# Seven block products for the second feed-forward's gate and up tiles, with the residual held in DRAM

## The chip, the cores and the metric

The kernel runs on one core of a Trainium2 chip. The metric is the device time of one execution in microseconds; of several executions the median is taken.

## The reference

One decoder layer for T = 1092 columns (1024 prompt tokens, 64 sample tokens, 4 zero columns), width 1024, in float32:

```
h = x + 0.5 * g1 * SwiGLU_1(rms(x) * (1 + sc1) + sh1)
u = rms(h) * (1 + sc2) + sh2
h = h + g2 * mixer(u)                  # attention and state space branches, then @ w_out
h = h + 0.5 * g3 * SwiGLU_2(rms(h) * (1 + sc3) + sh3)
y = final_rms(h)

def swiglu(u, w_in, w_out):            # w_in 1024 x 5632, w_out 2816 x 1024
    g, up = split(u @ w_in, 2)
    return (silu(g) * up) @ w_out
```

The change concerns SwiGLU_2 and the join between the mixer and it.

## The kernel before, in words

Activations lie with features on the 128 partitions and the columns in the free dimension. Every float32 operand of a large product is scaled by a power of two and split into two fp16 parts, hi and lo (`split`, L92: hi on ScalarE at L94, lo on VectorE at L95). A product of a 128-feature tile runs three passes per k-tile: hi x hi, hi x lo, lo x hi. The columns go in three chunks of CH = 364 (the last takes 360 after the first pass), so a `unit` (L165, matmuls at L171) over nk k-tiles is 9 nk matmuls of some 363 columns into one PSUM tile.

`Weights` (L99) walks a fixed list of weight groups: `fetch` issues the DMA of a group into one of two buffers `wf` (L114, on SP's queue), `measure` reduces its absolute maximum on VectorE (L88), GpSimd spreads that over the partitions (L81), and `split` makes `wh` and `wl`, of which there are two buffers each. A group is split one step ahead of its use and loaded and measured two ahead.

A feed-forward (`ffn`, L376) has 22 tiles of hidden features. `up(i)` (L382) makes one: two units of 8 k-tiles (gate, then up), 144 matmuls; ScalarE takes the silu of the gate (L387), VectorE multiplies (L390) and reduces the tile's maximum for the later split. The first two tiles (`up_two`, L400, matmuls at L181) go chunk by chunk of the columns, since the modulated norm arrives in chunks. Hidden tiles are grouped by PARTS = ((0,11),(11,18),(18,22)); `halves` splits a part, `down` (L436) multiplies it with w_out and adds to the residual `x`, which stays in SBUF; `last_part` (L461) does the last four k-tiles chunk by chunk and calls `after_chunk` for each.

Before the second feed-forward, `mixer_b` (L1211) multiplies the two branches, merges them and applies w_out: a first half with `unit`, and `last_part` for the second, whose `after_chunk` computes the reciprocal root mean square (`rstd_chunk`, L277, a chain of thirteen small VectorE operations) and `modulate_chunk` (L309: VectorE L322, ScalarE L325 and L327, VectorE L327 for each part of the eight k-tiles). The order of instructions on each engine is that of the program with a scheduler's priorities; each engine executes its own list in order.

Of the kernel before, what the change touches and what calls it, by code (L numbers as in the profile page):

```python
# [20 lines left out]
P = 128  # L21
# [4 lines left out]
PARTS = ((0, 11), (11, 18), (18, 22))  # L26
# [6 lines left out]
T = 3 * CH  # L33
EPS = 1e-6
# [14 lines left out]
class K:  # L49
    """State shared by the parts of the kernel."""  # L50


class Pool:
    """A tile pool whose tiles are named after their tags."""
# [14 lines left out]
def pow2_scale(k, m, pool=None, tag="sc", bufs=8):  # L69
# [4 lines left out]
    nc.vector.tensor_scalar(sc[:, 1:2], sc[:, 1:2], 2.0 ** -100, 2.0 ** -14, op0=ALU.max, op1=ALU.mult)  # L74
    nc.vector.reciprocal(sc[:, 0:1], sc[:, 1:2])
    return sc[:, 0:1], sc[:, 1:2]
# [15 lines left out]
def split(k, hi, lo, src, s):  # L92
    """hi + lo = s * src to 22 bits."""
# [5 lines left out]
class Weights:  # L99
    """The groups of weights in the order in which they are used: split one ahead, loaded and measured two ahead.  # L100
    The last group of a product, of twice the size, is kept in slots of the scope's own, aside from the ring."""
# [5 lines left out]
    def fetch(self):  # L107
        k = self.k
        src, nk, nm, *aside = self.order.pop(0)
        wf = []  # L110
        for part in [src[:, :nk // 2], src[:, nk // 2:]] if aside else [src]:
# [3 lines left out]
        self.fetched.append((wf, nm, bool(aside)))  # L115

    def measure(self):
# [5 lines left out]
        m = absmax(k, mx) if aside else mx[:, :1]  # L123
        self.loaded.append((wf, nm, aside, *pow2_scale(k, allmax(k, m))))
# [6 lines left out]
    def split(self):  # L131
        k = self.k
        wf, nm, aside, s, inv = self.loaded.pop(0)
        parts = []
        for f in wf:
# [5 lines left out]

    def ahead(self):
        """To be called when the use of a group ends, or by next()."""
# [16 lines left out]
def width(c, first):  # L160
    """Columns of chunk c that a pass takes: the zeros after the last token only need the first one."""
# [3 lines left out]
def unit(k, w, cols, act, nk):  # L165
    """One output tile: [P, 3, CH] of PSUM = sum over nk k-tiles of w[:, :, cols]^T act."""
# [9 lines left out]
def product(k, ps, w, cols, act, nk, c):  # L176
    """ps [P, CH] = chunk c of the columns of such a tile."""
# [6 lines left out]

def unit_chunk(k, w, cols, act, nk, c, sink, ps=None):
    """Such a chunk in its own bank, for sink(c, ps)."""
# [28 lines left out]
def ada_part(k, dr, part, queue=None, then=None):  # L215
    """mods[:, part * 8 + tile, sequence]: one part of the modulation."""
# [25 lines left out]
def norm_coef(k, i, gain):  # L242
    """Modulation i as u * s = n * A + B, with s a power of two: A, B and 1 / s."""
# [9 lines left out]
    s, inv = pow2_scale(k, allmax(k, bound), k.co, f"ns{i}", 1)  # L253
# [9 lines left out]
def square_sums(k, x, c):  # L263
    """The sums of squares of the columns of chunk c of x [P, KD, T]: PSUM [4 x 32 equal rows, CH / 4]."""
    nc = k.nc
    ss = k.pss.tile([P, 512], F32, tag="s")
    for kt, nk in GROUPS:
        sq = k.tmp()[:, :nk, :]
        nc.scalar.activation(sq, x[:, kt:kt + nk, c * CH:(c + 1) * CH], AF.Square)
# [15 lines left out]
    # the inverse square root: half the exponent's bits, then Newton's steps  # L285
# [16 lines left out]
def normalize_chunk(k, x, c, bc=None):  # L302
    """x[:, :, chunk c] to unit root mean square, in place."""
# [43 lines left out]

def scaled_gate(k, gate, iv):
# [5 lines left out]
def add_gated(k, xm, ps, g):  # L354
    """xm [P, T] += g * ps, g [P, NSQ] by sequence, ps [P, 3, CH]."""
# [1177 lines left out]
```

## Time and profile before

| quantity | value |
|---|---|
| median of three runs | 2511.44 us (2509.38, 2511.44, 2512.85) |
| profiled execution, its span | 2513.7 us |
| TensorE (PE) busy | 2430.5 us, 97%, 16615 matmuls |
| VectorE (DVE) busy | 1417.2 us, 56% |
| ScalarE (ACT) busy | 782.4 us, 31% |
| GpSimd (POOL) busy | 168.2 us, 7% |

The profile is one further execution; the page gives its span, which holds the program from the first instruction to the last, and shows no other time of it. Busy time is summed per engine. A matmul's listed duration holds its passage through the array as well, so the distance between the starts of successive matmuls is what a matmul costs in a stream.

### The profile page before, as it was taken

The numbers are of one execution on the slowest core, as the hardware profiler recorded it, in microseconds if no ns is written. First come the engines' busy times: TensorE is split into PE (matmuls) and PEld (weight loads), VectorE is DVE, ScalarE is ACT, GpSimd is POOL, SyncE is SP. The second block draws the span as 40 slices with busy tenths as digits, with TensorE's granted clock in tenths as the row PEclk, the third lists the DMA queues.
The fourth block names the chain that finished last, engine by engine and source line by source line (L and its number), as shares of the span: only waits on it lengthen the run. The fifth ranks groups of instructions, "written<-read, shape, count | busy, mean of one in ns | idle before, by whom it ended". The sixth has DMA issues, their size and how long they took to land.

```text
span 2513.7 us, 38505 instructions
## 1 busy us (share of the span) xinstructions
PE 2430.5 (97%) x16615; PEld 1456.6 (58%) x16615; DVE 1417.2 (56%) x2637; ACT 782.4 (31%) x905; POOL 168.2 (7%) x249
## 2 busy tenths in 40 slices
PE   6999999999999999999999899999999999999997
PEld 2555566666656565775444444655666656666564
DVE  4522355458676744638889787697333353333545
ACT  3311122111122432146778676324211221111303
POOL 0111000000000000001133200000000000000000
PEclk8999999999999999889999999999999999999999
DMA  9644101112112234444133214520111111111112
GB/s 349 220 184 168 51 24 55 62 62 88 59 57 99 89 98 147 104 149 157 66 110 104 96 41 148 210 68 18 34 51 51 36 47 62 51 48 35 45 35 72
DMA packets 81946, 229.41 MB, mean 91 GB/s; under 512 B 11680, under 2 KB 45856, under 8 KB 72560
## 3 DMA queue, kind: packets, MB, share of 16 engines
q1 hardware_dynamic: 67952, 179.96, 21.0%
q0 software_dynamic: 13376, 46.70, 5.3%
q8 instruction: 130, 2.13, 0.3%
q10 hardware_dynamic: 448, 0.29, 0.1%
q14 instruction: 40, 0.33, 0.0%
HBM read 190.68 MB, written 36.24 MB: 90 GB/s over the span
## 4 chain that ended last, share of the span: by engine, by line
PE 42%; DVE 6%; ACT 4%; issue 2%; DMA 1%; another core or an unknown queue 1%; POOL 0%; DVEq 0%; POOLq 0%; ACTq 0%
PE u L171 27%; PE u L181 8%; PE z L850 2%; PE o L868 1%; PE P L787 1%; DVE mx L88 1%; PE P L863 1%; DVE h L95 1%; DVE wl L95 1%; DMA wf<-in_w_in 0%; ACT tmp L325 0%; DMA wf<-in_w_out_b 0%; ACT ae L857 0%; PE z L911 0%
## 5 line engine op out<-in xcount | busy, mean ns | idle before, releaser
L171 PEld LDWEIGHTS <-wh 128*128 128x128 f16 x6144 | 589.3, 97 | 387.3 <-issue 38.5
L171 PE MATMUL u<-u,wh 128*128 128x364 f16 (+1 forms) x4032 | 740.6, 317 | 0.0
L171 PE MATMUL u<-u,wl 128*128 128x364 f16 (+1 forms) x2016 | 420.1, 315 | 0.0
L181 PE MATMUL u<-u,wh 128*128 128x364 f16 (+1 forms) x1632 | 393.5, 319 | 12.0 <-ACT u L327 6.3
L171 PEld LDWEIGHTS <-wl 128*128 128x128 f16 x3072 | 298.9, 98 | 176.1 <-issue 2.6
L94 ACT ACTIVATE wh<-wf,sc 128x2048 f16<-128x2048 f32 (+3 forms) x92 | 172.1, 1871 | 681.8 <-PE u L171 616.5
L88 DVE TENSOR_REDUCE mx<-wf 128x1 f32<-128x2048 f32 (+3 forms) x98 | 208.7, 2131 | 250.3 <-DMA wf<-in_ffn_w_in 156.6
L171 PE MATMUL u<-h,wh 128*128 128x364 f16 (+1 forms) x1728 | 315.7, 317 | 9.9 <-DVE h L95 6.1
L181 PE MATMUL u<-u,wl 128*128 128x364 f16 (+1 forms) x816 | 260.2, 319 | 1.1 <-DVE wl L95 1.1
L181 PEld LDWEIGHTS <-wh 128*128 128x128 f16 x1824 | 176.5, 98 | 126.0 <-issue 28.6
L390 DVE SCALAR_TENSOR_TENSOR h<-u,iv,sil 128x1092 f32<-128x1092 f32 x40 | 54.2, 1354 | 331.6 <-PE u L171 293.8
L95 DVE SCALAR_TENSOR_TENSOR wl<-wf,sc,wh 128x2048 f16<-128x2048 f32 (+3 forms) x92 | 200.7, 2182 | 47.3 <-ACT wh L94 46.8
L81 POOL PARTITION_ALL_REDUCE am<-mx x106 | 49.4, 472 | 1966.7 <-DVE mx L88 1880.2
L171 PE MATMUL u<-h,wl 128*128 128x364 f16 (+1 forms) x864 | 180.1, 316 | 0.0
L387 ACT ACTIVATE sil<-u,iv 128x1092 f32<-128x1092 f32 x40 | 46.9, 1171 | 385.3 <-PE u L171 385.3
L181 PEld LDWEIGHTS <-wl 128*128 128x128 f16 x912 | 89.4, 98 | 69.8 <-issue 18.5
L181 PEld LDWEIGHTS <-aside 128*128 128x128 f16 x864 | 83.0, 97 | 50.4 <-issue 1.2
L181 PE MATMUL u<-h,aside 128*128 128x364 f16 (+1 forms) x576 | 90.9, 317 | 0.0
L358 DVE SCALAR_TENSOR_TENSOR x<-u,gt,x 128x728 f32<-128x728 f32 x40 | 38.8, 971 | 87.7 <-PE u L171 87.7
L227 PE MATMUL s<-aw,cs 128*32 128x256 f32 x576 | 64.8, 406 | 11.2 <-DMA aw<-in_ada_w 11.1
L857 ACT ACTIVATE ae<-z,bias,csqk 128x512 f32<-128x512 f32 (+3 forms) x96 | 62.9, 666 | 40.7 <-PE z L855 18.8
L858 DVE TENSOR_SCALAR az<-z,csqk,bias 128x512 f32<-128x512 f32 (+3 forms) x96 | 64.4, 674 | 8.8 <-ACT ae L857 8.2
(375 smaller groups left out, 2583.5 us busy)
## 6 DMA issues: line engine op xcount, KB each, us to landing
wf<-in_ffn_w_in SPq DMA_DIRECT2D x44, 1024.0 KB, 4.9
aw<-in_ada_w POOLq DMA_DIRECT2D x56, 512.0 KB, 6.6
wf<-in_w_in SPq DMA_DIRECT2D x16, 1024.0 KB, 5.6
wf<-in_ffn_w_out_a SPq DMA_DIRECT2D x16, 704.0 KB, 4.1
x<-in_xT SPq DMA_DIRECT2D x6, 1456.0 KB, 14.1
sg<-gd SPq DMA_DIRECT2D x16, 546.0 KB, 5.5
aw<-in_ada_w SPq DMA_DIRECT2D x16, 512.0 KB, 8.3
gd<-gate SPq DMA_DIRECT2D x45, 182.0 KB, 1.9
```

The source lines that it names most:

```text
L81: k.nc.gpsimd.partition_all_reduce(r, m, P, ABSMAX)
L88: k.nc.vector.tensor_reduce(m, src, axis=axis, op=ALU.max, apply_absolute_value=True)
L94: r = k.nc.scalar.activation(hi, src, AF.Copy, scale=s)
L95: k.nc.vector.scalar_tensor_tensor(lo, src, s, hi, op0=ALU.mult, op1=ALU.subtract)
L171: k.nc.tensor.matmul(ps[:, c, :n], wt[:, cols], act(kt, part)[:, c * CH:c * CH + n], start=kt == 0 and j == 0, stop=kt == nk - 1 and j == 2)
L181: k.nc.tensor.matmul(ps[:, :n], wt[:, cols], act(kt, part)[:, c * CH:c * CH + n], start=kt == 0 and j == 0, stop=kt == nk - 1 and j == 2)
L227: nc.tensor.matmul(ps[32 * i:32 * i + 32, :], k.cs[:, 4 * kk + j, :], ws[i][:, j, :], start=kk + j == 0, stop=kk == 1 and j == 3)
L387: nc.scalar.activation(c3(sil), pg, AF.Silu, scale=iv)
L390: nc.vector.scalar_tensor_tensor(c3(h), pu, iv, c3(sil), op0=ALU.mult, op1=ALU.mult)
L850: nc.tensor.matmul(ps[:, :n], a[r, P * j:P * j + P], b[r, cols], start=i == 0, stop=True, skip_group_check=True)
L857: nc.scalar.activation(ae[:, h, :n], ps[:, :n], AF.Abs, scale=inv, bias=b)
L858: nc.vector.tensor_scalar(az[:, h, :n], ps[:, :n], inv, b, op0=ALU.mult, op1=ALU.add)
```

## The change

In the second feed-forward each gate and up tile is made from seven products of blocks (Winograd's form of Strassen's scheme): the k-tiles are cut into two halves of four, the columns into two halves of HT = 546, the outputs into gate and up. Each of the seven products has 4 k-tiles x 3 passes over 546 columns, in two matmuls of 272 and 274 columns: 24 matmuls, 168 for a tile where there were 144 of some 363 columns. Sums of products build up in PSUM where they can; the others are added on VectorE (`seven_products`). The weights' sums s1 to s4 are made on VectorE before the split (`Weights.seven`); the group's splits grow from 2048 columns to 2048, 1024 and 512. The activations' sums t1 to t4 are made in `Factors.chunk`, called for each of three chunks of 182 + 182 columns, and take the place of the modulated norm's buffer; the plain blocks lie in a new pool. `x` is stored to DRAM (`xd`) after the mixer, each row comes back for the first `down` and is stored again, and `x` is reloaded before the second. `halves_unit` cuts the columns in two halves for the mixer's branches and the down products, PSUM becomes three tiles of two banks, and PARTS becomes ((0,10),(10,18),(18,22)) for both feed-forwards.

```diff
-PARTS = ((0, 11), (11, 18), (18, 22))
+PARTS = ((0, 10), (10, 18), (18, 22))
...
+    def seven(self, f, s):
+        a11, a12, a22, a21 = (f[:, i:i + 512] for i in range(0, 2048, 512))
...
+        v.tensor_sub(s3, a11, a21)
+        v.tensor_add(a21, a21, a22)
+        v.tensor_sub(s2, a21, a11)
+        v.tensor_sub(s4, a12, s2)
+        h, l = (k.wp.tile([P, 2048], F16, tag=t_, bufs=2) for t_ in ("wh", "wl"))
+        split(k, h, l, f, s)
+        h3, l3 = (k.w3.tile([P, 1536], F16, tag=t_, bufs=2) for t_ in ("w3h", "w3l"))
+        split(k, h3[:, :1024], l3[:, :1024], t[:, :1024], s)
+        split(k, h3[:, 1024:], l3[:, 1024:], s4, s)
...
+def halves_unit(k, w, cols, act, nk):
+    for h in range(2):
+        ps = pair_tile(k)
+        cut = ((240, 512), (512, 786))
...
+    def chunk(self, k, x, coef, c, bc):
...
+        for g in range(4):
...
+            for q in range(2):
+                v.tensor_mul(t[:, q], paired(x, c)[:, 4 * q + g], bch)
...
+            v.tensor_sub(s[:, 0:2], flat[:, 1::2], flat[:, 0:2])
+            v.tensor_sub(s[:, 2], flat[:, 3], s[:, 0])
+            v.tensor_sub(s[:, 3], flat[:, 2], s[:, 2])
+            for src, hi, lo in ((flat[:, 0], ...
+                nc.scalar.activation(hi, src, AF.Copy)
+                v.tensor_sub(lo, src, hi)
...
+def seven_products(k, w, fac, iv, h, lo, hi):
...
+    add(X, "a11", "b11", True)
+    nc.scalar.activation(p1, view(X), AF.Copy)
+    add(Y, "s2", "t2", True)
+    v.tensor_add(u2, view(Y), p1)
+    add(X, "a12", "b21", False)
+    nc.scalar.activation(h1, view(X), AF.Silu, scale=iv)
+    add(Y, "s3", "t3", False)
+    v.tensor_add(u3, view(Y), p1)
+    add(Z, "s1", "t1", True)
+    v.tensor_add(u3, view(Z), u3)
+    add(Y, "a22", "t4", False)
+    v.tensor_add(p1, view(Y), p1)
+    add(Z, "s4", "b22", False)
+    v.tensor_add(h2, view(Z), u2)
+    nc.scalar.activation(h2, h2, AF.Silu, scale=iv)
+    v.scalar_tensor_tensor(hh, q[:, :, :n], iv, hh, op0=ALU.mult, op1=ALU.mult)
...
+    def up_two():
...
+        for lo, hi in ((0, 2 * QT), (2 * QT, HT)):
+            for i in range(2):
+                seven_products(k, ws[i][0], fac, ivs[i], hs[i], lo, hi)
...
+    def row(m):
+        t = k.hp.tile([P, T], F32, tag="h", name="xr")
+        nc.sync.dma_start(t, xd[:, m, :])
+        return t, lambda: nc.sync.dma_start(xd[:, m, :], t)
...
+    for m in range(KD):
+        nc.sync.dma_start(x[:, m, :], xd[:, m, :])
...
+                box["fac"] = Factors(k)
+            box["fac"].chunk(k, x, box["cf"], c, rstd_chunk(k, x, c, pairs=True))
+            nc.sync.dma_start(paired(xd, c), paired(x, c))
```

VectorE's list around one of the later tiles, before (`wf` raw weights, `wl` their lo part, `am` the spread maximum, `h` the hidden tile, L88 maxima):

```order
L390 SCALAR_TENSOR_TENSOR h<-u,iv,sil 128x1092
L88 TENSOR_REDUCE hm<-h 128x1
L95 SCALAR_TENSOR_TENSOR wl<-wf,sc,wh 128x2048
L88 TENSOR_REDUCE mx_17449<-wf 128x1
L73 TENSOR_SCALAR sc<-am 128x1
```

One multiplication, one maximum and one split, and then the maximum of the weights that have just been loaded.

And in the changed kernel, from the last add of a tile's products to the first add (`u2`, printed as u_17933, L494) of the next tile, for which TensorE's next product into the same PSUM tile waits (L97 is the lo part of a split, L90 a maximum, L508 the hidden tile):

```order
L503 TENSOR_TENSOR q<-u,q 128x546
L97 SCALAR_TENSOR_TENSOR wl<-wf,sc,wh 128x2048
L505 TENSOR_TENSOR h<-u,u_17721 128x546
L97 SCALAR_TENSOR_TENSOR w3l<-tmp,sc,w3h 128x1024
L508 SCALAR_TENSOR_TENSOR h<-q,iv,h 128x1092
L97 SCALAR_TENSOR_TENSOR w3l<-tmp,sc,w3h 128x512
L90 TENSOR_REDUCE hm<-h 128x1
L90 TENSOR_REDUCE mx_17921<-wf 128x1
L494 TENSOR_TENSOR u_17933<-u,q 128x546
```

Where one product's result and one split stood per tile, there are seven operations between the add that follows the a22 product (L503) and the next tile's `u2`.

VectorE's list at the start of the second feed-forward, before (L327 to L343 finish the last chunk of the norm, L417 multiplies the first two tiles' chunks):

```order
L340 TENSOR_TENSOR tmp<-tmp,B 128x512
L327 TENSOR_TENSOR u<-tmp,u 128x3x296
L343 TENSOR_TENSOR u<-tmp,u 128x8x64
L327 TENSOR_TENSOR u<-tmp,u 128x2x296
L417 SCALAR_TENSOR_TENSOR h<-u,iv,sil 128x364 x4
```

The last chunk's part of the norm is followed at once by the first tiles' multiplications.

And in the changed kernel (L454 to L461 finish the last chunk of the activations' sums and their lo parts, L155 to L158 make the weights' sums of a later tile, L494 is the first tile's first add):

```order
L454 TENSOR_TENSOR tmp<-tmp 128x364
L461 TENSOR_TENSOR f<-tmp,f 128x182
L455 TENSOR_TENSOR tmp<-tmp 128x182
L461 TENSOR_TENSOR f<-tmp,f 128x2x182
L456 TENSOR_TENSOR tmp<-tmp 128x182
L461 TENSOR_TENSOR u<-tmp,u 128x4x182
L155 TENSOR_TENSOR tmp<-wf 128x512
L156 TENSOR_TENSOR wf<-wf 128x512
L157 TENSOR_TENSOR tmp<-wf 128x512
L158 TENSOR_TENSOR tmp<-wf,tmp 128x512
L494 TENSOR_TENSOR u_16661<-u,q 128x364
```

The first tile's first pass takes 364 of each half's 546 columns, which come from the first two chunks; its first add stands behind the last of the third chunk's operations and four weights' sums.

## Rows read from the trace of the kernel before

**Rows 1.** The page: busy time, share of the span and instructions of each engine.
```profile
PE 2430.5 (97%) x16615; PEld 1456.6 (58%) x16615; DVE 1417.2 (56%) x2637; ACT 782.4 (31%) x905; POOL 168.2 (7%) x249
```
**Rows 2.** Windows from the mixer's branches on: us, busy (count) per engine, PEclk, DMA.
```profile
1599.00:1694.70 95.70, 91.92 (x593) 56.90 (x591) 84.37 (x112) 27.50 (x21) 5.38 (x7) 1.00 0.29 100
1694.70:1745.40 50.70, 49.92 (x426) 30.69 (x424) 39.43 (x83) 23.65 (x30) 0.69 (x2) 1.00 0.07 22
1745.40:1794.30 48.90, 47.45 (x357) 29.60 (x357) 20.16 (x37) 14.92 (x22) 0.00 (x0) 1.00 0.04 13
1794.30:2016.40 222.10, 222.10 (x1442) 139.47 (x1441) 76.95 (x92) 36.98 (x26) 4.26 (x12) 1.00 0.13 46
```
**Rows 3.** The chain of waits, 1590 to 2400: start us, us, what.
```profile
1764.66 29.61 PE u L181 x192
1794.27 222.15 PE u L171 x1440
...
2016.51 1.35 DVE h L390
2017.87 1.27 DVE h L95
...
2019.18 345.58 PE u L171 x2229
...
2368.68 7.60 DVE h L95 x6
```
**Rows 4.** Timeline of PE in the mixer's projection: start us, us, instruction.
```profile
1058.85 0.27 PE L1107 MATMUL z<-wl,u 128*128 128x256 f16 x1
...
1059.83 0.27 PE L1107 MATMUL z<-wl,u 128*128 128x256 f16 x1
```
**Rows 5.** Groups by line and shape, ACT, 1580 to 2380: busy us, mean ns, idle.
```profile
L94 ACT ACTIVATE wh<-wf,sc 128x2048 f16<-128x2048 f32 x26 | 52.0, 2001 | 218.5 <-PE u L171 196.9 <-PE u L181 11.5 <-DVE sc L75 10.1
L325 ACT ACTIVATE tmp<-tmp,B,A 128x364 f32<-128x364 f32 x16 | 9.9, 678 | 13.4 <-DVE tmp L322 13.4
```
**Rows 6.** The same view of DVE.
```profile
L95 DVE SCALAR_TENSOR_TENSOR wl<-wf,sc,wh 128x2048 f16<-128x2048 f32 x26 | 60.9, 2344 | 9.3 <-ACT wh L94 9.0
L88 DVE TENSOR_REDUCE mx<-wf 128x1 f32<-128x2048 f32 x26 | 59.4, 2285 | 89.0 <-DMA wf<-in_ffn_w_in 87.9 <-DMA wf<-in_w_out_b 1.1
L88 DVE TENSOR_REDUCE hm<-h 128x1 f32<-128x1092 f32 x22 | 28.4, 1289 | 0.6
L390 DVE SCALAR_TENSOR_TENSOR h<-u,iv,sil 128x1092 f32<-128x1092 f32 x20 | 27.1, 1355 | 185.4 <-PE u L171 185.4
...
L477 DVE SCALAR_TENSOR_TENSOR x<-u,gs,x 128x364 f32<-128x364 f32 x16 | 8.7, 590 | 2.4 <-PE u L181 2.2
...
L290 DVE TENSOR_TENSOR r<-r 128x91 f32<-128x91 f32 x9 | 2.3, 256 | 0.3
...
L295 DVE TENSOR_TENSOR rd<-r,ident 128x364 f32<-128x364 f32 x3 | 1.6, 537 | 0.1
...
L322 DVE TENSOR_TENSOR tmp<-x,s 128x592 f32<-128x592 f32 x1 | 0.8, 762 | 0.0
...
L482 DVE TENSOR_TENSOR st<-u,gs 128x192 f32<-128x192 f32 x2 | 0.7, 351 | 0.0
...
L338 DVE TENSOR_TENSOR tmp<-x,s 128x512 f32<-128x512 f32 x1 | 0.7, 679 | 0.0
```
**Rows 7.** Timeline around one tile's end: SP's DMA issue, then the maximum and its wait.
```profile
1843.77 0.33 SPq L114 DMA_DIRECT2D wf<-in_ffn_w_in  x1
...
1848.60 2.29 DVE L88 TENSOR_REDUCE mx<-wf 128x1 f32<-128x2048 f32 x1 [4.85 <-DMA wf<-in_ffn_w_in]
```
**Rows 8.** Windows of PE around two of its pauses: us, busy (count), PEclk, DMA share, GB/s.
```profile
2016.00:2019.20 3.20, 0.89 (x7) 0.97 0.00 0
2019.20:2021.00 1.80, 1.80 (x7) 0.50 0.00 0
2021.00:2023.00 2.00, 2.00 (x10) 0.65 0.00 0
2384.00:2389.00 5.00, 3.38 (x23) 1.00 0.00 0
```

More of the change, by code (lines that the diff above doesn't have):

```diff
@@ L33 @@
 T = 3 * CH
+HT = T // 2
+QT = HT // 3
 EPS = 1e-6
@@ L49 @@
 class K:
+    pass
 class Pool:
@@ L182, in product, with paired, two, pair_tile @@
                                start=kt == 0 and j == 0, stop=kt == nk - 1 and j == 2)
+def paired(t, c):
+    if len(t.shape) == 2:
+        return t.rearrange("p (h c n) -> p c h n", h=2, c=3)[:, c]
+    return t.rearrange("p k (h c n) -> p k c h n", h=2, c=3)[:, :, c]
+def two(t):
+    return t.rearrange("p (h n) -> p h n", h=2) if len(t.shape) == 2 else t.rearrange("p k (h n) -> p k h n", h=2)
+def pair_tile(k):
+    return k.psu.tile([P, 1024], F32, tag="u", bufs=3)
+def halves_unit(k, w, cols, act, nk):
+    for h in range(2):
+        ps = pair_tile(k)
+        cut = ((240, 512), (512, 786))
+        for kt in range(nk):
+            for j, (wt, part) in enumerate(passes(w, kt)):
+                for a, b in cut:
+                    a0 = h * HT - 240
+                    k.nc.tensor.matmul(ps[:, a:b], wt[:, cols], act(kt, part)[:, a0 + a:a0 + b],
+                                       start=kt == 0 and j == 0, stop=kt == nk - 1 and j == 2)
+        yield h, slice(h * HT, h * HT + HT), ps[:, 240:786]
 def unit_chunk(k, w, cols, act, nk, c, sink, ps=None):
@@ L485, in last_part, with ffn_seven, hidden, up @@
         after_chunk(c)
+def ffn_seven(k, fac, ivu, gate, xd, after_chunk):
+    nc = k.nc
+    hs, hm = {}, {}
+    def hidden(i):
+        p = [a <= i < b for a, b in PARTS].index(True)
+        if p not in hm:
+            hm[p] = k.small.tile([P, 12], F32, tag="hm", bufs=3)
+        j = i - PARTS[p][0]
+        return hm[p][:, j:j + 1]
+    def up(i):
+        w = k.w.next()
+        iv = mul_small(k, w[1], ivu)
+        hs[i] = k.hp.tile([P, T], F32, tag="h")
+        seven_products(k, w[0], fac, iv, hs[i], 0, HT)
+        absmax(k, hs[i], hidden(i))
+    def up_two():
+        ws = [k.w.next() for _ in range(2)]
+        ivs = [mul_small(k, w[1], ivu) for w in ws]
+        for i in range(2):
+            hs[i] = k.hp.tile([P, T], F32, tag="h")
+        for lo, hi in ((0, 2 * QT), (2 * QT, HT)):
+            for i in range(2):
+                seven_products(k, ws[i][0], fac, ivs[i], hs[i], lo, hi)
+        for i in range(2):
+            absmax(k, hs[i], hidden(i))
+    def halves(p):
+        a, b = PARTS[p]
+        s, inv = pow2_scale(k, allmax(k, absmax(k, hm[p][:, :b - a])), tag="sh", bufs=3)
+        parts = []
+        for i in range(a, b):
+            h2 = k.hp.tile([P, 2, T], F16, tag="h")
+            ins = split(k, h2[:, 0, :], h2[:, 1, :], hs[i], s)
+            if i - a < 6:
+                behind = ins
+            parts.append(h2)
+        return lambda kt, part: parts[kt][:, part, :], inv, behind
+    def down(p, hact, inv, behind, rows):
+        nk = PARTS[p][1] - PARTS[p][0]
+        per = 1 + p
+        for m in range(KD):
+            if m % per == 0:
+                if m == 0:
+                    with k.tc.issue_after(behind):
+                        w = k.w.next()
+                else:
+                    w = k.w.next()
+                iv = mul_small(k, w[1], inv)
+            xm, done = rows(m)
+            g = scaled_gate(k, gate[:, m, :], iv)
+            for h, _, ps in halves_unit(k, w, slice(m % per * P, m % per * P + P), hact, nk):
+                add_gated_half(k, xm, h, ps, g)
+            done()
+    def row(m):
+        t = k.hp.tile([P, T], F32, tag="h", name="xr")
+        nc.sync.dma_start(t, xd[:, m, :])
+        return t, lambda: nc.sync.dma_start(xd[:, m, :], t)
+    up_two()
+    for i in range(2, PARTS[0][1] + 1):
+        up(i)
+    down(0, *halves(0), row)
+    for i in range(PARTS[0][1] + 1, NFF):
+        up(i)
+    x = k.up.tile([P, KD, T], F32, tag="u", name="x")
+    for m in range(KD):
+        nc.sync.dma_start(x[:, m, :], xd[:, m, :])
+    h1, h2 = halves(1), halves(2)
+    down(1, *h1, lambda m: (x[:, m, :], lambda: None))
+    last_pairs(k, x, gate, *h2, lambda c: after_chunk(c, x))
```

222 lines of the change are left out of this document (172 added, 50 removed).

## The prediction, made before the changed kernel had run

> **What bounds the kernel now.** The page first: TensorE is busy 97% of the span and VectorE 56% [rows 1], so on average the matmul stream is the bound, and a scheme that needs fewer matmul columns attacks the right engine. Averages hide stages, so next the windows from the mixer's branches on [rows 2]. In the second feed-forward's plain tiles (1794.3 to 2016.4) TensorE is busy without a gap while VectorE works 76.95 of 222.1 us. In the branches and the first half of w_out (1599.0 to 1694.7) VectorE is already busy 84.37 of 95.7 us, and in the next two windows, the chunked product with the norm behind it and the first two tiles, it works 39.43 of 50.7 and 20.16 of 48.9 us: there it is close behind TensorE. The chain of waits says the same: one piece of 222.15 us of matmuls for ten tiles, a break of 2.7 us where the hidden tile and its split end last (2016.51 to 2019.18), then 345.58 us of matmuls [rows 3]. The last column but two of the windows is the granted clock, 1.00 in all of these.
>
> **What TensorE saves.** Ten tiles are 1440 matmuls in 222.15 us: 22.2 us a tile, 154.3 ns for some 363 columns [rows 3]. For 272 or 274 columns no row stands; the nearest are the projection's 256-column matmuls, each with a weight load of its own: nine starts in 0.98 us, 108.9 ns [rows 4]. A line through both gives 0.424 ns a column, almost nothing fixed, and 116.1 ns for 273 columns. A tile of 168 then takes 19.5 us, 2.7 less; for the 20 tiles after the first two **-54 us**. Weight loads (139.47 us for 1441, 97 ns each [rows 2]) still fit behind matmuls of 116 ns. The down products change from 9 x 154.3 to 12 x 116.1 ns a k-tile, 144 k-tiles: +0.6 us.
>
> The Trainium skill, page "TensorE: Matmul & The Clock Gate", section "Back-to-back issue gap", speaks against this: in a stream of weight loads and matmuls it gives about 81 ns for 128 columns and 131 ns for 512. Read linearly that is an estimate of 100 and 112 ns here, so a tile would go from 16.1 to 16.8 us and the change would lose on TensorE itself. The trace does not agree: 363 columns take 154.3 ns, more than the page has for 512, and 256 and 363 columns stand nearly in proportion.
>
> **What VectorE must do in a later tile.** It gets 15 us of work a tile (four adds of 512 columns 2.4, five of 546 columns 3.2, splits 4.1, the hidden product 1.3, two maxima 3.4, small ones 0.8) where it has 7.7 (76.95 us for ten [rows 2]); that would hide under 19.5 us, but the order matters. Take the end of the a22 product as zero. It frees the weights' slot, so ScalarE's `wh` runs until 2.05 (2.00 us [rows 5]). VectorE's list then stands in a row; successive operations start 0.08 us before the listed end of the one ahead (six splits of 1.35 us take 7.60 [rows 3]). `wl` to 4.45 (2.34), h2's add of 546 columns 0.64 net (0.76 at 592), to 5.09; `w3l` of 1024 columns 1.20, to 6.29 (between 0.59 at 364 and 2.34 at 2048); the hidden product 1.27, to 7.56; `w3l` of 512 columns 0.67, to 8.23; the tile's maximum 1.21, to 9.44 [rows 6]. The next weights' DMA starts after `wl` and takes 4.85 us [rows 7], landing at 9.33, in time; their maximum 2.21, to 11.65; then u2's add, to **12.3**. TensorE has four products of 24 matmuls (s4 b22, and the next tile's first three) before it needs that add: 4 x 2.79 = **11.15**. It waits 1.15 us in each such tile. The tiles whose successors' weights are narrow w_out groups are free of it (two before each down product), as is the first, priced below; 15 remain: **+17 us**. Bounds: 0, if the eight operations of this list are 0.15 us shorter each, and 2.3 us a tile if the DMA is late by as much as ScalarE's turn. I take 1.15, which the rows give.
>
> **The join.** Here VectorE loses what TensorE gains.
> - Window 1: two weight groups' sums and extra splits come in: four adds of 512 columns (0.68, net 0.60 [rows 6]) and 1.20 + 0.67, 4.3 us a group, 8.6 for two, and 1 us for operations cut in halves. VectorE is idle 11.3 us of this window; I let half of the addition fall into that: +5.4 (0 to 9.6).
> - From there TensorE's first chunk ends after 16.9 us, a third of 50.7 [rows 2]. Then VectorE is never free until the first u2 add, since its list holds all three chunks' sums ahead of it, though the first pass only needs two. A chunk's sums are four groups of two multiplications of 364 (0.46 net each), adds of 364, 182 and 182 (0.46, 0.27, 0.27) and lo parts of 182, 364 and 728 (0.27, 0.46, about 0.84) [rows 6]: 3.5 us a group, 14 a chunk, 16 in the third with the sample columns. Before, the norm took some 7. With three root-mean-square chains (thirteen operations at 0.25, the first exposed at some 6 us), two chunks' residual adds (eight at 0.52, some more for samples: 4.5 and 5) and four weights' adds: 6 + 14 + 4.5 + 3.3 + 14 + 5 + 3.3 + 16 + 3 = 69 us. ScalarE has 3.5 us a group as well (0.68 for one 364 [rows 5]; two of those and three conversions) in alternation with VectorE's; I allow 10 us for the two waiting for each other (2 to 18). The u2 add ends 96 us after window 1.
> - TensorE has done 36 matmuls of the first pass by then and waits. What is left: 132 at 154.7, 20.4 us; 168 of 182 columns, between 77 ns by the line and 97 by their weight loads, 14.6 us; a wait of 2.5 in the second pass, where a weight split (`wl` 2.3 and `w3l`) stands ahead of the second tile's add. After a pause of 2.7 us the clock was granted at 0.50 and came back after some 3 us, a loss of 1.6 us, while a pause of 1.6 us left it at 1.00 [rows 8]; this pause is longer, so +1.6. That is 39 us.
> - 96 + 39 = 135 against 99.6 before: +36, with window 1 **+41 us** (29 to 55).
>
> **Small terms.** The third tile's weights are split late: +2. At the break before the first down product, an add of 0.64 and a silu of some 0.7 join the 2.7 us chain: +1.2. The last chunk's paired output: +0.5. Storing and reloading x runs on SP's queue while TensorE works: the first row is needed only after a half-unit of 7 us, and weights' loads behind it are two groups ahead; 0, or about 5 us (one load's 4.85 [rows 7]) if a row comes late at either down product. The waits of 1.15 us are shorter than the pause that left the clock alone, so they cost no clock. FFN 1's new parts: 0.
>
> **The sum.** -54 + 17 + 41 + 0.6 + 2 + 1.2 + 0.5 = +8 us on the profiled span of 2513.7, which lies 2.3 above the median of the runs: 2511.4 + 8 = 2520, and with the x traffic's bound in view I say **2521 us**, slower by 0.4%. Below 0.2%, or 5 us, a measurement cannot tell a change.
>
> **Rivals.**
> - *VectorE keeps up* (faster). If u2's add ends before 11.15 in the later tiles, the 17 us fall away, and if VectorE and ScalarE interleave well the join costs 32: 2521 - 17 - 9 = 2495. It decides at 1.15 us in a list of 12.3. For it: VectorE idles some 4 us of every tile in my walk, behind `wh` and the products. Against: its list is in order and the wait for `wh` is given by the slots. Chance 0.20.
> - *One of the two comes out well*: 2504 or 2512. Chance 0.17.
> - *The waits cost clock.* If each is 2.6 us in place of 1.15, the clock falls to 0.50 as after the 2.7 us pause: 1.45 + 1.6 us in 15 tiles, 46 us: 2567. For it: a DMA or ScalarE 1.4 us late suffices. Chance 0.08.
> - *Seven products are no fewer.* If matmuls of 273 columns do not start every 116 but every 131 ns, 168 of them take 22.0 us, as the 144 did. VectorE's wait vanishes too: 2521 + 50 - 17 = 2554. The proportion of rows 3 and 4 speaks against it. The page named above has a rule of this kind. Chance 0.05.
>
> **How the numbers follow.** My forecast has 0.50, with a range of its own of 2510 to 2538 from the join's bounds; 2521 is its middle. Faster by over 0.2% (below 2506.4): the first rival and a little of the second, 0.23. Within: the rest of the second and the forecast's low end, 0.19. Slower: 0.58. For eight in ten the range goes from 2494, the first rival's time, to 2545, where the join's upper bound ends; the two dear rivals and half of the cheap one stay outside.
>
> **What would show it.** Right: matmuls of 272 and 274 columns start about 116 ns apart; in the list of waits PE waits for DVE at L494 some 1.2 us a tile, and a tile takes 20.6 us; between the end of the w_out product and the first two tiles PE pauses for 20 us or more, released by the L494 add, and VectorE is full meanwhile; the later tiles begin some 41 us later than before. Wrong: tiles of 19.5 us without a wait (first rival), a granted clock below 1.00 in the later tiles (third), a spacing well above 116 (fourth), or waits of PE at the down products for the adds that need x.

## Result, and the profile after

| | us |
|---|---|
| changed kernel, median of 6 runs | 2525.93 (2521.8 to 2534.3) |
| kernel before, same chip, 6 runs | 2511.68 (2509.38 to 2519.49) |
| ratio, 95% interval | 1.0058 [1.0038, 1.0078] |
| span of the profiled execution | 2522.0, before 2513.7: +8.3 |

The change makes the kernel slower by 0.6%. The forecast was 2521 us, slower, and +8 us on the profiled span. The direction is right and the two spans differ as forecast, but the medians differ by 14.2 us (13.7 in the repeat below), so the change costs more than I said. The terms agree less well still, as shown below.

The page's first line now (it answers to [rows 1]): TensorE has 44 us less, VectorE 194 us more.

```profile
PE 2386.3 (95%) x17863; PEld 1577.3 (63%) x17863; DVE 1611.6 (64%) x3008; ACT 850.8 (34%) x1029; POOL 163.4 (6%) x249
```

What TensorE waited for, 1480 us to the end, changed kernel: engine and line that waited, who released it, total us, times, longest.

```profile
PE u L481 <- ACT q L491: 18.6, 2, 18.2
PE u L481 <- DVE u L494: 12.6, 17, 2.3
PE u L237 <- DMA ob<-od: 12.4, 2, 11.5
```

These three lines are the largest of the change's new waits. The first is one pause of 18.2 us in the join; the second 0.7 us in each of most later tiles; the third, at the start of the mixer's branches, is nowhere in the prediction.

The chain of waits of the changed kernel (it answers to [rows 3]): start, us, what.

```profile
1709.47 14.87 PE u L539 x96
...
1949.84 19.77 PE u L481 x167
1969.62 19.89 PE u L481 x168
...
2029.09 105.19 PE u L237 x898
...
2163.30 8.28 PE u L481 x69
...
2183.89 8.28 PE u L481 x69
...
2204.46 8.28 PE u L481 x69
...
2361.18 89.81 PE u L237 x768
2451.00 14.60 PE u L539 x95
```

Three marks split the path: the last half of w_out begins at 1709.47 (before: 1694.9), the third tile of the second feed-forward at 1837.1 (before: 1794.27 [rows 3]), the last half of the last product at 2451.00 (before: 2446.3). A tile for which the list shows no wait takes 19.9 us, 118.4 ns a matmul (19.89 us for 168); with its wait a tile recurs every 20.58 us (2163.30, 2183.89, 2204.46). The 20 tiles and their down products take 613.9 us where they took 652.0, a gain of 38.1; everything ahead of them had already lost 42.8. The third tile has no clean start: 19 of its matmuls run ahead of the mark, and twelve of the second tile's with a wait of 1.4 us behind it, which come to 2.2 and 2.3 us and nearly cancel.

The 118.4 ns still hold a piece of the wait. In a tile without a listed wait `u2` ends at 1969.57, and the product that needs it starts at 1969.62, 0.40 us after the start of the last two matmuls ahead of it, where two otherwise take 0.23:

```profile
1968.85 0.72 DVE L494 TENSOR_TENSOR u<-u,q 128x546 f32<-128x546 f32 x1
1969.22 0.39 PE L481 MATMUL u<-f,wl 128*128 128x272 f16 x2
1969.62 0.63 PE L481 MATMUL u<-u,w3h 128*128 128x272 f16 x4
```

The 0.16 us too much lie within the last matmul's listed duration and so in no list of waits. A tile without any wait takes 19.7 us, as a run below shows.

Windows of the changed kernel (columns as in [rows 2]): the join up to TensorE's restart, the last 6 us of that, the rest of the first two tiles, and the following tiles.

```profile
1709.40:1803.00 93.60, 66.85 (x538) 38.56 (x537) 81.51 (x215) 47.91 (x83) 0.69 (x2) 0.84 0.22 60
1797.00:1803.00 6.00, 4.02 (x15) 2.00 (x15) 4.57 (x8) 3.00 (x4) 0.00 (x0) 0.57 0.00 0
1803.00:1837.10 34.10, 33.14 (x294) 25.44 (x293) 16.45 (x26) 7.48 (x13) 0.00 (x0) 1.00 0.09 32
1837.10:2010.00 172.90, 167.34 (x1419) 137.17 (x1417) 128.70 (x174) 49.85 (x52) 3.88 (x11) 1.00 0.14 49
```

VectorE is busy 81.51 of the join's 93.6 us, TensorE only 66.85. In the plain tiles VectorE works 74% of the time, where it worked 35% [rows 2].

How the pause ends is seen in the timelines of the changed kernel, each row with the wait ahead of it in brackets. ScalarE, where the copy of the first product (L491) stands behind the third chunk's last conversion:

```profile
1797.56 0.81 ACT L460 ACTIVATE u<-tmp 128x728 f16<-128x728 f32 x1 [1.19 <-DVE tmp L456]
1798.28 0.46 ACT L491 ACTIVATE q<-u 128x364 f32<-128x364 f32 x1
```

VectorE, from the third chunk's last lo part to the first `u2`:

```profile
1798.41 0.92 DVE L461 TENSOR_TENSOR u<-tmp,u 128x728 f16<-128x728 f32 x1 [0.88 <-ACT u L460]
1799.24 0.68 DVE L155 TENSOR_TENSOR tmp<-wf 128x512 f32<-128x512 f32 x1
...
1802.02 0.53 DVE L494 TENSOR_TENSOR u<-u,q 128x364 f32<-128x364 f32 x1
```

And TensorE:

```profile
1798.79 0.76 PE L481 MATMUL u<-f,wh 128*128 128x364 f16 x2 [18.16 <-ACT q L491]
...
1802.61 0.47 PE L481 MATMUL u<-u,w3h 128*128 128x364 f16 x2 [0.19 <-DVE u L494]
```

TensorE had made two products by then. The third goes into the PSUM tile that ScalarE must copy first. After it the `u2` add is only 0.19 us late.

### The profile page after: what moved, and what is told of

Read it like the earlier page. It is cut to its first block, busy times and chain, and to the rows that moved or that the text cites. A ratio compares the mean times of both kernels' runs of the same rounds, so it can differ in the third digit from the quotient of the medians.

```text
span 2522.0 us, 41583 instructions
## 1 busy us (share of the span) xinstructions
PE 2386.3 (95%) x17863; PEld 1577.3 (63%) x17863; DVE 1611.6 (64%) x3008; ACT 850.8 (34%) x1029; POOL 163.4 (6%) x249
## 4 chain that ended last, share of the span: by engine, by line
PE 35%; DVE 11%; ACT 4%; issue 2%; DMA 2%; another core or an unknown queue 1%; POOL 0%; DVEq 0%; ACTq 0%; POOLq 0%
PE u L237 11%; PE u L481 10%; PE u L208 5%; PE u L539 2%; PE z L1138 2%; DVE wl L97 2%; DVE mx L90 1%; ACT wh L96 1%; PE o L1156 1%; PE P L1075 1%; DVE w3l L97 1%; PE P L1151 1%; DVE h L508 1%; DVE hm L90 1%
## 5 line engine op out<-in xcount | busy, mean ns | idle before, releaser
L96 ACT ACTIVATE wh<-wf,sc 128x2048 f16<-128x2048 f32 (+2 forms) x92 | 172.1, 1870 | 646.8 <-PE u L198 287.2
L208 PE MATMUL u<-u,wh 128*128 128x364 f16 (+1 forms) x1440 | 347.3, 318 | 11.1 <-ACT u L387 6.3
L198 PE MATMUL u<-u,wh 128*128 128x364 f16 (+1 forms) x1920 | 357.8, 317 | 0.0
L90 DVE TENSOR_REDUCE mx<-wf 128x1 f32<-128x2048 f32 (+2 forms) x98 | 208.7, 2130 | 164.5 <-DMA wf<-in_ffn_w_in 77.9
L97 DVE SCALAR_TENSOR_TENSOR wl<-wf,sc,wh 128x2048 f16<-128x2048 f32 (+2 forms) x92 | 201.0, 2185 | 64.5 <-ACT wh L96 62.9
L208 PE MATMUL u<-u,wl 128*128 128x364 f16 (+1 forms) x720 | 229.0, 318 | 1.1 <-DVE wl L97 1.1
L198 PE MATMUL u<-u,wl 128*128 128x364 f16 (+1 forms) x960 | 200.7, 316 | 0.0
L198 PEld LDWEIGHTS <-wl 128*128 128x128 f16 x1392 | 134.9, 98 | 79.7 <-issue 2.2
L237 PE MATMUL u<-h,wh 128*128 128x272 f16 (+1 forms) x1152 | 181.7, 279 | 1.0 <-DVE h L97 0.9
L198 PE MATMUL u<-h,wh 128*128 128x364 f16 (+1 forms) x864 | 157.3, 317 | 5.2 <-DVE h L97 3.5
L481 PE MATMUL u<-f,wh 128*128 128x272 f16 (+2 forms) x704 | 115.5, 282 | 20.6 <-ACT q L491 18.6
L481 PE MATMUL u<-u,w3h 128*128 128x272 f16 (+2 forms) x704 | 114.8, 281 | 15.5 <-DVE u L494 12.6
L208 PEld LDWEIGHTS <-wl 128*128 128x128 f16 x816 | 79.5, 97 | 63.4 <-issue 17.7
L481 PE MATMUL u<-u,wh 128*128 128x272 f16 (+2 forms) x704 | 115.9, 280 | 0.0
## 6 DMA issues: line engine op xcount, KB each, us to landing
x<-in_xT SPq DMA_DIRECT2D x6, 1456.0 KB, 13.7
```

The lines of the kernel that those rows point to most:

```text
L90: k.nc.vector.tensor_reduce(m, src, axis=axis, op=ALU.max, apply_absolute_value=True)
L96: r = k.nc.scalar.activation(hi, src, AF.Copy, scale=s)
L97: k.nc.vector.scalar_tensor_tensor(lo, src, s, hi, op0=ALU.mult, op1=ALU.subtract)
L198: k.nc.tensor.matmul(ps[:, c, :n], wt[:, cols], act(kt, part)[:, c * CH:c * CH + n], start=kt == 0 and j == 0, stop=kt == nk - 1 and j == 2)
L208: k.nc.tensor.matmul(ps[:, :n], wt[:, cols], act(kt, part)[:, c * CH:c * CH + n], start=kt == 0 and j == 0, stop=kt == nk - 1 and j == 2)
L237: k.nc.tensor.matmul(ps[:, a:b], wt[:, cols], act(kt, part)[:, a0 + a:a0 + b], start=kt == 0 and j == 0, stop=kt == nk - 1 and j == 2)
```

## Experiments

Every run stands beside runs of the kernel before on the same chip. To place a gain in time, three stretches are read from each profile: from the end of the last attention projection to the last half of w_out (140.8 us before, 157.9 after), from there to the last half of the last product (751.4 before, 741.5 after), and from there to the end (67.4 before, 71.0 after). Between profiles of kernels whose edits lie elsewhere, the first stretch varies from 157.1 to 160.0 us with the change, and the middle one from 741.0 to 744.7; less than some 4 us in one of them shows nothing.

**The later tiles' wait.** VectorE's list between two tiles' products (changed kernel) shows why `u2` is late: one operation after the other, and the weights' maximum right ahead of it.

```profile
2171.84 0.73 DVE L503 TENSOR_TENSOR q<-u,q 128x546 f32<-128x546 f32 x1 [2.09 <-PE u L481]
2173.69 2.35 DVE L97 SCALAR_TENSOR_TENSOR wl<-wf,sc,wh 128x2048 f16<-128x2048 f32 x1 [1.12 <-ACT wh L96]
...
2179.72 1.28 DVE L90 TENSOR_REDUCE hm<-h 128x1 f32<-128x1092 f32 x1
2180.92 2.28 DVE L90 TENSOR_REDUCE mx<-wf 128x1 f32<-128x2048 f32 x1
2183.11 0.72 DVE L494 TENSOR_TENSOR u<-u,q 128x546 f32<-128x546 f32 x1
```

Two edits take one operation each out of that row. First the hidden tile's maximum (`hm`, 1.2 us net):

```diff
-        absmax(k, hs[i], hidden(i))
+            k.late.append(lambda: absmax(k, hs[i], hidden(i)))
...
-    v.tensor_add(u2, view(Y), p1)
+    first = v.tensor_add(u2, view(Y), p1)
+    if k.late:
+        with k.tc.issue_after(first.ins):
+            k.late.pop()()
```

> The maximum of a hidden tile (1.2 us of VectorE) is put behind the next tile's first add u2. If u2 is late because of VectorE's own list, PE's waits at u2 (15 times, some 0.72 us in the usual tile) vanish and the time falls by about 11 us. Rival, the row of events is wl, then the weights' DMA of 4.85 us, then the maximum of the new weights, then u2: taking 1.2 us out of the list only makes VectorE wait for the DMA, the waits shrink by 0.1 us each, and the time falls by at most 2 us. I hold the rival for the likelier here.

Measured: 2518.1 us, ratio 1.006 [1.0041, 1.0078]. TensorE still waits 11.0 us in 16 tiles for L494, and the middle stretch is 742.4 us: no gain. VectorE's timeline of this kernel says why:

```profile
2199.20 2.29 DVE L90 TENSOR_REDUCE mx<-wf 128x1 f32<-128x2048 f32 x1 [1.02 <-DMA wf<-in_ffn_w_in]
2201.40 0.72 DVE L494 TENSOR_TENSOR u<-u,q 128x546 f32<-128x546 f32 x1
```

VectorE now reaches the weights' maximum 1.0 us before the weights have landed, and idles. The DMA, which starts after `wl`, stood close behind the row of operations and becomes the limit.

Second, the weights' maximum itself, and with it the wait for the landing:

```diff
-            self.fetch()
-            self.measure()
+            self.fetch()
+            if not self.lazy:
+                self.measure()
...
+    if k.w.fetched:
+        with k.tc.issue_after(first.ins):
+            k.w.measure()
```

> The maximum of the newly loaded weights (2.2 us) is put behind the next tile's u2 instead. Both readings of the waits say that u2 is then ready before TensorE needs it: waits under 0.1 us, tiles of 19.8 us in place of 20.6, the time down by about 11 us (span near 2511). Rival, the late split (ScalarE's wh, which waits for the slot) or the adds of products set the tile: waits of 0.5 us or more stay, and the time falls by less than 4 us.

Measured: 2503.07 us, ratio 1.001 [0.9995, 1.0024], against 1.0061 for the change on another chip. In TensorE's list of waits 0.6 us are left of the 12.6 (the add is L496 in this kernel):

```profile
PE u L483 <- DVE u L496: 0.6, 2, 0.4
```

The middle stretch is 727.0 us, 14.5 less. Eleven tiles are now one piece of the chain:

```profile
2119.93 217.00 PE u L483 x1848
```

That is 117.4 ns a matmul, 19.7 us a tile. The listed waits were 12.0 of the gain; the 0.16 us of each tile that no list shows make some 3 more in 20 tiles. The sum of 15 agrees with the 14.5 within what the stretch varies.

**The join.** Two edits on the three additions that make t1 to t4. One gives them to GpSimd:

```diff
-            v.tensor_sub(s[:, 0:2], flat[:, 1::2], flat[:, 0:2])
-            v.tensor_sub(s[:, 2], flat[:, 3], s[:, 0])
-            v.tensor_sub(s[:, 3], flat[:, 2], s[:, 2])
+            nc.gpsimd.tensor_sub(s[:, 0:2], flat[:, 1::2], flat[:, 0:2])
+            nc.gpsimd.tensor_sub(s[:, 2], flat[:, 3], s[:, 0])
+            nc.gpsimd.tensor_sub(s[:, 3], flat[:, 2], s[:, 2])
```

> The activations' sums t1 to t4 (three of VectorE's eight operations in a group, 1.0 of 3.5 us, 12 us over the three chunks) are made on GpSimd. If VectorE's work fills the join, the first u2 comes 8 to 12 us earlier (it stood at 1802) and the time falls by about 9 us. Rival, VectorE and ScalarE wait for each other: GpSimd's slower sums lengthen each group, the first u2 comes no more than 2 us earlier or later than before, and the time stays or rises.

Measured: 2526.99 us, ratio 1.0102 [1.0077, 1.0127]; the middle stretch is 750.9 us, 9.4 more. GpSimd's groups of that kernel in the join:

```profile
L454 POOL TENSOR_TENSOR tmp<-tmp 128x364 f32<-128x364 f32 x12 | 11.2, 930 | 54.8 <-ACT tmp L442 36.5 <-ACT tmp L445 18.3
L456 POOL TENSOR_TENSOR tmp<-tmp 128x182 f32<-128x182 f32 x12 | 8.8, 732 | 0.9
L455 POOL TENSOR_TENSOR tmp<-tmp 128x182 f32<-128x182 f32 x12 | 6.4, 536 | 0.9
```

The three take 2.2 us a group on GpSimd; on VectorE they took 0.54 + 0.34 + 0.34. ScalarE's conversions wait for them (17.1 us in twelve waits; for VectorE's sums they waited 12.6 us in eleven), and VectorE's lo parts wait for those. The sums lie in the chain, so handing them to a slower idle engine does not shorten the join.

GpSimd's own pace is not the only possible cause. VectorE's lo parts that run beside the additions became slower too, first in the changed kernel, then in this run:

```profile
L461 DVE TENSOR_TENSOR f<-tmp,f 128x182 f16<-128x182 f32 x12 | 4.1, 342 | 0.0
L461 DVE TENSOR_TENSOR f<-tmp,f 128x182 f16<-128x182 f32 x12 | 10.2, 849 | 1.6 <-ACT f L460 1.6
```

Those of 364 columns went from 531 to 814 ns, so VectorE spent 9.5 us more on the two kinds together. How much of the 9.4 us comes from this and how much from GpSimd's slower additions, no run here separates.

The other edit leaves the three additions out: the lo and hi parts of t1 to t4 are then made from the plain blocks, so the gate and up tiles of this run are not the reference's.

```diff
-            v.tensor_sub(s[:, 0:2], flat[:, 1::2], flat[:, 0:2])
-            v.tensor_sub(s[:, 2], flat[:, 3], s[:, 0])
-            v.tensor_sub(s[:, 3], flat[:, 2], s[:, 2])
-                                (s, *(self.t[:, :, g, i, cols] for i in range(2)))):
+                                (flat, *(self.t[:, :, g, i, cols] for i in range(2)))):
```

> Leaves out the three additions that make t1 to t4 in each group of the activations (the plain blocks are converted in their place). VectorE has 12 x 1.2 us less to do in the join. If VectorE's list fills the join, the first u2 comes about 13 us earlier after the start of L539 (93 us before) and the stretch from L539 to the last four k-tiles falls by about 13 us. Rival, ScalarE's conversions in alternation with VectorE set it: less than 6 us.

Beside it the change itself once more:

> The changed kernel once more, beside the others on one chip. Ratio to the kernel before 1.006, from the last projection matmul ahead of the branches to the start of the second half of w_out (L539) 158 us, from there to the last four k-tiles of the second feed-forward 741 us.

Measured: 2503.47 us, ratio 1.0012 [0.9999, 1.0026], against 2514.94 us, 1.0061 [1.0044, 1.0079], for the change: 11.5 us. The change's own repeat has 160.0, 742.9 and 71.0 us in the three stretches. The middle stretch falls from 742.9 to 729.4 us. In the list of waits of the run without the additions, TensorE's pause is shorter:

```profile
PE u L477 <- ACT q L487: 13.4, 2, 13.0
```

So the sums on VectorE, and what waits for them, do set the join. The pause shrank by 5.1 us, and TensorE goes on 77.3 us after the start of the last half of w_out (1778.04 less 1700.7) in place of 88.6 (1786.58 less 1698.0): 11.3 of the 13.5 us lie ahead of that point.

What stands last ahead of the first add are four weights' sums. They were moved behind the first tiles' first pass:

```diff
-        ws = [k.w.next() for _ in range(2)]
+        ws = [k.w.ready.pop(0) for _ in range(2)]
...
+            if not lo:
+                k.w.split()
+                k.w.load()
```

> The changed kernel with one edit: the third weight group's sums and splits stand behind the first tiles' first pass, so that VectorE's four sums (2.8 us) leave the place ahead of the first u2 add. Theory: TensorE's pause of 18.2 us stays, since the copy of the first product on ScalarE ends it and not the add; only the 0.2 us wait for the add goes, and from the start of the last half of w_out to that of the last product 741.5 us become 741 to 742. Rival: the four sums hold the pause up, and it shrinks to about 15.5 us, the stretch to 738.

In one run the middle stretch is 741.7 us. The add now ends 90.1 us after the start of the last half of w_out, 3 us sooner than in the changed kernel; but TensorE's timeline shows the pause unchanged, which makes ScalarE's copy its end and not the add:

```profile
1796.24 0.77 PE L481 MATMUL u<-f,wh 128*128 128x364 f16 x2 [18.15 <-ACT q L491]
```

**The wait at the branches.** `ob`, the second branch's activations, comes back from DRAM. Before the change its four loads were issued from 1545.4 to 1547.0, in the changed kernel from 1557.5 to 1561.7 (the view by tile; columns: ns min/median/max, first and last start):

```profile
L1507 SPq DMA_DIRECT2D ob<-od x4: 320/372/432, 1557.5 to 1561.7; - x4
```

The first theory was SP's order, since loads of `sg` stand ahead of them there. The edit puts them behind `ob`:

```diff
-                    nc.sync.dma_start(sg, gd[8 * branch + m])
+                with k.tc.issue_after(load.ins) if branch else nullcontext():
+                    nc.sync.dma_start(sg, gd[8 * branch + m])
```

> The four loads of the second branch's operand (ob) are queued on SP ahead of the loads of the gates (sg). If the queue's order cost the join 11.5 us of PE waiting for ob, that wait goes, the second half of the w_out product (L539 in the changed kernel) starts some 7 us earlier than 1709.5, and the time falls by about 7 us against the changed kernel (span 2522.0, median 2526). Rival, VectorE sets the end of this window anyway: the PE wait goes, but L539 starts at most 2 us earlier and the time falls by 0 to 2 us.

Measured: 2518.91 us, ratio 1.0075 [1.0051, 1.0099]. The first stretch is 158.6 us, no shorter, and the theory falls. The four issues now lie between 1533.9 and 1554.8:

```profile
L1507 SPq DMA_DIRECT2D ob<-od x4: 320/371/424, 1533.9 to 1554.8; - x4
```

The first goes out at 1533.92, the other three from 1553.92 on. What holds them is in the list of waits of SP's queue for this run (L97 is the lo part of a split), and VectorE's timeline has the split that ends then, at 1553.89:

```profile
SPq L1507 <- DVE u L97: 19.6, 1, 19.6
```

```profile
1548.76 5.13 DVE L97 SCALAR_TENSOR_TENSOR u<-qT,so,u 128x1088 f16<-128x1088 f32 x4
```

It reads the attention's queries `qT`, and it stands just ahead of the branches. In the changed kernel the same four splits end at 1560.85, and the second load of `ob` goes out at 1560.88:

```profile
1555.72 5.13 DVE L97 SCALAR_TENSOR_TENSOR u<-qT,so,u 128x1088 f16<-128x1088 f32 x4
```

The change put `ob` into the pool of the plain blocks (six slots). A load that waits for the last reader of `qT` fits slots that lie over `qT`; the addresses themselves stand in no view. The next edit keeps the order of the loads and divides the pool in four and two slots, to give `ob` memory over the keys alone:

```diff
-                    k.fac.tile([P, 2, 2, HT], F16, tag="f", bufs=6) for _ in range(2)]
+                    k.fac.tile([P, 2, 2, HT], F16, tag="f2", bufs=2) for _ in range(2)]
...
-    k.fac.tile([P, 2, T], F16, tag="f", bufs=6, name=n)
+    k.fac.tile([P, 2, T], F16, tag="f", bufs=4, name=n)
```

> The four ob tiles get slots of their own in the pool, which lie over the keys alone and not over the queries (which VectorE splits until just before the branches), and their loads stand ahead of the gates' loads. Theory: the 9 to 12 us for which PE waits for ob come from the slots' memory; the wait falls below 3 us, and the stretch from the last projection to L539 falls from 158 to about 149 us, the time by 9 us against the changed kernel. Rival: the gates (sg) or VectorE then set the branches, the stretch stays above 155 us.

Measured: 2508.67 us, ratio 1.0029 [1.0009, 1.0049], 6.3 us below the change beside it, where 9 were expected; the two intervals are wide enough for either. The four issues lie between 1535.6 and 1536.9, and the first stretch is 148.4 us, 9.5 less than after the change. In TensorE's list of waits the DMA is gone; what it waits for at that place (the first line) was there in the kernel before (the second):

```profile
PE u L237 <- ACT gate L1408: 2.4, 1, 2.4
PE u L171 <- ACT gate L1120: 2.4, 1, 2.4
```

**Small terms.** The new grouping of the hidden tiles, alone, in the kernel before:

```diff
-PARTS = ((0, 11), (11, 18), (18, 22))
+PARTS = ((0, 10), (10, 18), (18, 22))
```

> The kernel before with nothing of the change but the new grouping of hidden tiles, 10, 8 and 4 in place of 11, 7 and 4, in both feed-forwards. Theory: the grouping costs and gives nothing, since the matmuls are the same; ratio 0.999 to 1.001, and the mixer's projection ends where it did, at 1554.0 us. Rival: the 2.5 us by which the projection ends earlier in the changed kernel (1551.5) come from the first feed-forward's grouping; ratio 0.998 or 0.999, with the end of the projection 2 to 3 us earlier.

Measured: 2512.66 us, ratio 1.0002 [0.9987, 1.0018]. The grouping costs and gives nothing that these runs can tell. The end of the projection came at 1561.2 in this profile, of an execution that took 2523.5 us, the longest of ten; over the profiles here it lies between 1538.0 and 1561.2, so the 2.5 us between before and after at that place mean nothing.

The output's store takes its columns in pairs of 182, which cuts its rows. A contiguous tile ahead of it:

```diff
-                nc.vector.tensor_mul(t, t, bc.unsqueeze(1).to_broadcast([P, 2, 2, QT]))
-                nc.sync.dma_start(two(out["y"][c, :, kt:kt + 2]), t)
+                o = k.tmp().rearrange("p a n -> p (a n)")[:, :4 * QT].rearrange("p (k n) -> p k n", k=2)
+                nc.vector.tensor_mul(two(o), t, bc.unsqueeze(1).to_broadcast([P, 2, 2, QT]))
+                nc.sync.dma_start(out["y"][c, :, kt:kt + 2], o)
```

> The changed kernel with one edit: the final result goes through a contiguous tile before it is stored, so that the store's pieces are long again. Theory: the 71.0 us from the start of the last half of the last product to the end of the span come back to 67.9 or less (before: 67.4), since the short pieces of the last store cost about 3.1 us. Rival: the paired columns of the whole tail cost, not the store; then it stays above 70.

In one run the last stretch is 67.1 us, 3.9 less. The packets that the DMA moved in the last 26 us, in the kernel before:

```profile
DMA packets 2177, 3.00 MB, mean 115 GB/s; under 512 B 128, under 2 KB 2176, under 8 KB 2176
```

In the changed kernel they were half as long, 0.7 KB on average in place of 1.4:

```profile
DMA packets 3108, 2.22 MB, mean 85 GB/s; under 512 B 97, under 2 KB 3106, under 8 KB 3106
```

and with the contiguous tile they are longer than before the change, 2.6 KB:

```profile
DMA packets 1154, 3.01 MB, mean 116 GB/s; under 512 B 128, under 2 KB 128, under 8 KB 1152
```

**A kernel faster than both.** The slots and order of `ob`, the late maximum of the weights, the contiguous store and the third group's late sums together, all as shown above:

> The maximum of new weights behind u2, ob in slots that lie over the keys alone and loaded first, the third tile's weight sums behind the first pass of the first two tiles, the result's last pieces made contiguous before they are stored. By the theory -14 for the first, -9 for ob, -3 for the weight sums, -3 for the store against the changed kernel: about 29 us, ratio to the kernel before some 0.994. Rival: the parts hide behind one another (VectorE in the branches, ScalarE in the join), and only the first counts: ratio 1.000 to 1.001.

Measured: 2490.22 us (7 runs), ratio 0.9961 [0.9949, 0.9972], 24.7 us below the change beside it, where some 29 were expected. Its middle stretch is 727.3 us, its last 67.0, and nearly eight of the later tiles stand in its chain without a break:

```profile
1833.90 153.80 PE u L483 x1308
```

The pause in the join is still there:

```profile
PE u L483 <- ACT q L493: 18.6, 2, 18.2
```

## Why the prediction was right, step by step

- **The total: the direction right, the size too small.** The two spans differ by 8.3 us where I said +8, and that is luck. By the marks above, the part up to the third tile is 1.8 us dearer than my terms, the tiles and their down products 4.9 us cheaper, the tail 3.1 dearer. It is also luck of one execution: by the medians the change costs 14.2 us, and in the repeat the three stretches alone add up to +14.3. A run's time is 2.1 us more than its span (2524.14 for 2522.0), which I did not allow for, so the profiled execution of the kernel before stands, by estimate, for 2515.8 us, 4 above its median. The upper ends of my ranges, 2538 and 2545, do not follow from the join's bound either: 55 in place of 41 gives 2535.
- **What TensorE saves: a little too much.** I took 116.1 ns for a matmul of 273 columns from a line through two widths. It is 117.4 in the tiles of the run with the late maximum (217.00 us for 1848) and 116.9 in the last down product (89.81 us for 768). A tile without wait costs 19.7 us in place of 19.5, so 20 tiles save 50 and not 54 us; the down products cost some 2 us more and not 0.6. The rival of 131 ns is out. The other rule on the page "TensorE: Matmul & The Clock Gate" of the Trainium skill (section "Wait — 56ns, not 53.3ns?"), N / 2.4 GHz + 2.5 ns, gives an estimate of 116.3; the trace agrees within 1.2 ns, where the page's sustained figures (section "Back-to-back issue gap"), read linearly, gave 100.
- **The later tiles' wait: mechanism right, size 0.86 for 1.15.** From the end of the a22 product to the end of `u2` I walked 12.3 us; the timeline has 12.2 (about 2171.65 to 2183.83). What was off is the other side: four products of 24 matmuls at 117.4 ns are 11.3 us, not 11.15. A usual tile recurs every 20.58 us, 0.86 more than 19.72: 0.7 in the list and 0.16 hidden. My 20.6 for it came out because both its parts were off. In all 12.5 us are listed and some 3 hidden, where I had 17. I also held the two tiles ahead of each down product free of it because their successors' groups were narrow; the groups of the second down product are not (8 x 256 columns), and the longest of these waits, 2.27 us, stands there. That VectorE's list sets the wait is shown by the late maximum (the wait nearly vanishes), and that the DMA stands just behind it by the run with the late `hm`.
- **Breaks.** I charged 2 us for the third tile and 1.2 for the break before the first down product. TensorE waits 0.9 us for the split there, where it had paused 2.7 [rows 3]. The tile stretch's 38.1 us are the saved 50 less some 16 of waits and some 2 for the down products, which leaves about 6 us gained at breaks. Most of that can be read: apart from L494, TensorE waits 2.3 us in the stretch where it waited 5.7 before, and the clock, which before the change fell to 0.50 after the pause at 2019 [rows 8] (I priced that at 1.6), stays at 1.00.
- **The join: sum right, composition wrong.** Predicted +41 up to the third tile, measured +42.8. Against the projection's end the last half of w_out comes 17.1 us later, not 5.4. The wait for `ob` is 11.54 us in place of 2.4. Its product takes 48.8 us in place of 44.9, with a second wait of 0.9 in it and the clock granted at 0.50 for some 7 us after the pause (rows in the last section). Only the remaining 4.0, by difference, are left for the weights' sums, which I had priced at 5.4; with the wait for `ob` gone, the same part is 5.1 us longer than before. The step that failed is the one on small terms: I looked for DMA trouble where `x` is stored and reloaded, and not at where the pool of the plain blocks lies and who reads that memory last. The wait for `ob` is in no term of mine; it costs 9.5 us by the run that removes it. From there on I was too dear: `u2` ends 93 us after the last half of w_out begins (96 predicted), and the third tile starts 34.6 us later (39 predicted), because matmuls of 182 columns start 78.8 ns apart (I took up to 97), the wait in the second pass is 1.4 us and not 2.5, and the slow clock falls on twelve matmuls that end just as `u2` does. So +28 stands where I had +36, and the two errors, some +12 and -8, nearly cancel; with the projection 2.5 us earlier in this execution that makes +42.8.
- **Who ends the pause.** I named the L494 add. It is ScalarE's copy L491, behind the same third chunk on its own list; the add is 0.19 us late behind it. The place and the cause were right, VectorE's and ScalarE's alternation over three chunks.
- **The tail: +3.6 us where I had 0.5,** nearly all of it the store's short pieces: with the contiguous tile both runs that have it come to 67.
- **Clock.** No later tile lost clock: the windows from 1803 on stand at 1.00, as I held likelier.

Not tried is what holds the first pass behind the third chunk: the lists alone, or also memory, since the first adds' tiles may lie over buffers that the third chunk still uses.

## What to carry to other kernels

Fewer matmul columns pay only as far as the engine that makes their operands keeps up: here 50 us of TensorE's time came free, and more than that went again, 28 of it in the one stage where the additions stood on the path and some 16 where they delayed the next tile's first add. Put a reduction for a later group behind the add that the next product waits for; that one move was worth 14.5 us here. And when a change moves a buffer into another pool, look up which memory it now lies over and who reads that last: a load can wait there for an engine that has nothing to do with it.

## What the runs showed of the hardware

- Windows of the changed kernel behind the wait for `ob` (columns as above), from TensorE's first matmul on:

```profile
1563.00:1566.00 3.00, 2.07 (x9) 1.24 (x10) 0.00 (x0) 0.00 (x0) 0.00 (x0) 0.50 0.99 364
1566.00:1570.00 4.00, 4.00 (x20) 2.61 (x19) 0.00 (x0) 0.00 (x0) 0.00 (x0) 0.50 1.01 422
1570.00:1612.30 42.30, 42.30 (x363) 35.04 (x362) 19.21 (x26) 9.85 (x9) 0.70 (x2) 1.00 0.68 235
```

- So a pause of 11.5 us left the granted clock at 0.50, the lower of the two levels, for the next 7 us, and one of 18.2 us at 0.57 on average from 1797 to 1803; then it was 1.00. The twelve matmuls of 364 columns after the second pause took 302 ns each (1798.79 to about 1802.42), against 154.3 for 363 before [rows 3].
- Pauses of 2.4 us ahead of the branches had no fixed outcome: behind them the granted clock stood at 1.00 in the kernel before (1556.4 to 1562) and in the run with all edits together (1548.6 to 1555), and at 0.50 from 1550 to 1552 in the run with `ob` in slots of its own.
- Matmuls of 182 columns, each with a weight load of its own of 97 ns in the list, start 78.8 ns apart (24 in 1.89 us): a load's listed duration is no bound on the spacing.
- The same add of 364 float32 columns takes 0.93 us on GpSimd and 0.54 on VectorE; of 182 columns 0.54 to 0.73 and 0.34. GpSimd's figures were taken while VectorE worked beside it, and VectorE's own subtractions of 182 and 364 columns took 0.85 and 0.81 us there, where alone they take 0.34 and 0.53.
